# The down projection of a feed-forward as seven of eight block products, with its operands moved

## The chip, the cores and the metric

The kernel runs on one core of a Trainium2 chip. The metric is device time in microseconds (us) of one execution, the median of several runs. A core has a matrix engine (TensorE: PE for its matmuls, PEld for its weight loads), VectorE (DVE), ScalarE (ACT), GpSimd (POOL) and SyncE (SP), which here issues nearly all DMAs. Each engine works through its own list of instructions in order and waits on semaphores for the others. TensorE's results go to PSUM tiles of 128 x 512 float32, of which the kernel has eight; the other tiles lie in SBUF, 128 partitions wide.

## The reference, cut to what matters

Two layers, each with a feed-forward, a mixing sub-layer and a second feed-forward, on 512 tokens of width 1024, in float32. The feed-forward, used four times, is what changes:

```python
def _swiglu(h, wg, wu, wd):
    return (jax.nn.silu(h @ wg) * (h @ wu)) @ wd
...
    for i in range(DEPTH):
        h = _rmsnorm(x, ffn1_norm[i])
        x = x + 0.5 * _swiglu(h, ffn1_w_gate[i], ffn1_w_up[i], ffn1_w_down[i])
        h = _rmsnorm(x, mix_norm[i])
        x = x + _mixing(h, positions, w_in[i], w_out[i], fox_b, lbs[i], hgrn_norm)
        h = _rmsnorm(x, ffn2_norm[i])
        x = x + 0.5 * _swiglu(h, ffn2_w_gate[i], ffn2_w_up[i], ffn2_w_down[i])
    return _rmsnorm(x, final_norm)
```

The hidden width is 2816, 22 blocks of 128.

## The kernel before, in words

Everything is kept transposed: x is eight tiles x0 to x7 of 128 features by 512 tokens. A float32 product is made of three matmuls on operands of the rounded type fp32r: each operand is split into a rounded part (xh, wh, hh) and a rest (xl, wl, hl), and `mm3` (lines 248 to 252) adds high by high, high by low and low by high into one PSUM tile. Each weight block is loaded by SyncE into `raw` (three buffers), rounded to `wh` by ScalarE and subtracted to `wl` by VectorE (`load_split`, lines 233 to 246; two buffers each).

`ffn` (line 360) has two stages. **Gate/up**: for each of 22 blocks j, two groups (gate and up) of 8 x 3 matmuls of 512 columns into `gu_ps`; VectorE multiplies by the row factor rb, ScalarE takes the Silu, VectorE multiplies both, and the result is split into hh and hl (lines 376 to 385). **Down**: for each of the eight output blocks d, 22 x 3 matmuls of 512 columns into `d_ps`, with weights in three loads of 8, 7 and 7 blocks (line 390), and one addition of half of it to x (line 394). `after(d)` (line 395) then splits and squares that block of x for the next stage, whose first matmuls follow the last of the down stage without waiting for the norm.

The mixing stage between the feed-forwards has the same kind of projections of 512 columns (lines 250 to 252 and 425 to 427) and, among them, small matmuls in full precision (a_ps, ho_ps, ob_ps, lv_ps and others).

The order on each engine is made by the framework when the program is built: it lays out each engine's instructions by the order of the code, by when their operands can be there, and by a priority; `high_priority(AHEAD)` in `load_split` draws the splitting of weights ahead. At run time the order is fixed.

Tiles get their addresses in the order of the pools. In the built program xh, xl, wh and wl start 64 bytes past a multiple of 256, hh and hl 192 bytes past one; `pad` (48 floats) sets this.

## Time and profile before

| | us |
|---|---|
| median of 3 runs (2109.0 to 2109.46) | 2109.24 |
| profiled execution | 2108.85 |
| its span | 2107.1 |
| PE busy | 2080.3 |
| DVE busy | 993.5 |
| ACT busy | 691.6 |
| POOL busy | 13.0 |

The span is the time between the first and the last instruction of the profiled execution. A matmul's busy time contains its way through the array, which overlaps with the next one, so the busy time of PE is no sum of prices; the distance between starts is. Times inside the trace count from the start of the span.

### The profile page before, as it was taken

To read this page: it belongs to the slowest core of one execution; us is meant where nothing else is said; L and a number is where in the kernel's file an instruction comes from. 1 tells how busy PE (TensorE), PEld (TensorE's weight loads), DVE (VectorE), ACT (ScalarE), POOL (GpSimd) and SP (SyncE) were. 2 spreads that over 40 slices of the span, in tenths; PEclk is the share of its full clock that TensorE was granted. 3 is DMA by queue.
4 is the path that set the end of the run, shared out by engine and by line. 5 is a ranking of instruction groups with operands and counts; after the bars stand their busy time and mean duration, and the time that the engine had idled before them with its cause. 6 is when DMAs were issued, how large, how long until landed. Compare 5 with 4: busy or idle time off the path is not lost.

```text
span 2107.1 us, 23700 instructions
## 1 busy us (share of the span) xinstructions
PE 2080.3 (99%) x9622; PEld 1688.9 (80%) x9622; DVE 993.5 (47%) x1590; ACT 691.6 (33%) x1005; POOL 13.0 (1%) x18
## 2 busy tenths in 40 slices
PE   8999999999999999999999999999999999999997
PEld 6888888888777888888888888888887778888885
DVE  7444433556364544443344443336554554444323
ACT  5323222333353423222233322232344443323221
POOL 0000000000000000000000000000000000000000
PEclk9999999999999999999999999999999999999998
DMA  5322333211122222233332223332211122222332
GB/s 166 100 91 99 95 93 94 94 60 51 50 69 67 97 92 99 100 94 92 95 98 93 100 96 91 99 100 70 65 57 51 56 85 90 100 98 92 95 96 69
DMA packets 54373, 184.35 MB, mean 87 GB/s; under 512 B 6888, under 2 KB 7016, under 8 KB 54264
## 3 DMA queue, kind: packets, MB, share of 16 engines
q1 hardware_dynamic: 53656, 181.73, 27.1%
q8 instruction: 75, 1.23, 0.2%
q10 hardware_dynamic: 576, 1.05, 0.1%
q14 instruction: 34, 0.28, 0.0%
q0 software_dynamic: 32, 0.07, 0.0%
HBM read 180.69 MB, written 2.10 MB: 87 GB/s over the span
## 4 chain that ended last, share of the span: by engine, by line
PE 97%; DVE 2%; ACT 1%; DMA 0%; issue 0%; SPq 0%; DVEq 0%
PE gu_ps L252 15%; PE gu_ps L251 15%; PE gu_ps L250 15%; PE d_ps L252 8%; PE d_ps L250 8%; PE d_ps L251 8%; PE lv_ps L501 2%; PE sc_ps L552 2%; PE po L571 2%; PE o_ps L250 1%; PE o_ps L251 1%; PE o_ps L252 1%; PE ho_ps L680 1%; PE pt_ps L564 1%; PE v_ps L425 1%; PE v_ps L426 1%
## 5 line engine op out<-in xcount | busy, mean ns | idle before, releaser
L243 ACT CAST wh<-raw 128x1024 fp32r<-128x1024 f32 (+2 forms) x350 | 357.6, 1022 | 1112.7 <-issue 417.4
L245 DVE TENSOR_TENSOR wl<-raw,wh 128x1024 fp32r<-128x1024 f32 (+2 forms) x350 | 415.5, 1187 | 321.5 <-ACT wh L243 319.4
L250 PE MATMUL gu_ps<-xh,wh 128*128 128x512 f32 x1408 | 548.8, 390 | 7.5 <-ACT wh L243 7.5
L252 PE MATMUL gu_ps<-xh,wl 128*128 128x512 f32 x1408 | 550.4, 391 | 0.0
L251 PE MATMUL gu_ps<-xl,wh 128*128 128x512 f32 x1408 | 548.3, 390 | 0.0
L250 PEld LDWEIGHTS gu_ps<-xh,wh 128*128 128x128 f32 x1408 | 264.9, 188 | 63.6 <-ACT wh L243 7.5
L252 PEld LDWEIGHTS gu_ps<-xh,wl 128*128 128x128 f32 x1408 | 264.8, 188 | 56.1 <-issue 1.0
L251 PEld LDWEIGHTS gu_ps<-xl,wh 128*128 128x128 f32 x1408 | 264.8, 188 | 55.4 <-DVE xl L184 0.2
L252 PE MATMUL d_ps<-hh,wl 128*128 128x512 f32 x704 | 278.1, 395 | 0.0
L250 PE MATMUL d_ps<-hh,wh 128*128 128x512 f32 x704 | 278.1, 395 | 0.0
L251 PE MATMUL d_ps<-hl,wh 128*128 128x512 f32 x704 | 278.1, 395 | 0.0
L380 DVE TENSOR_TENSOR u<-gu_ps,rb 128x512 f32<-128x512 f32 x88 | 60.8, 691 | 269.2 <-PE gu_ps L252 269.0
L252 PEld LDWEIGHTS d_ps<-hh,wl 128*128 128x128 f32 x704 | 132.1, 188 | 32.2
L251 PEld LDWEIGHTS d_ps<-hl,wh 128*128 128x128 f32 x704 | 132.1, 188 | 32.1
L250 PEld LDWEIGHTS d_ps<-hh,wh 128*128 128x128 f32 x704 | 132.1, 188 | 32.1
L377 DVE TENSOR_TENSOR g<-gu_ps,rb 128x512 f32<-128x512 f32 x88 | 60.8, 691 | 178.7 <-PE gu_ps L252 176.6
L383 ACT CAST hh<-u 128x512 fp32r<-128x512 f32 x88 | 54.8, 623 | 61.2 <-DVE u L381 61.2
L394 DVE SCALAR_TENSOR_TENSOR x<-d_ps,x 128x512 f32<-128x512 f32 x32 | 22.1, 692 | 95.3 <-PE d_ps L252 95.3
L381 DVE TENSOR_TENSOR u<-u,g 128x512 f32<-128x512 f32 x88 | 60.9, 692 | 8.4
L501 PEld LDWEIGHTS lv_ps<-hQ,hk 128*128 128x128 f32 x448 | 55.8, 191 | 8.7 <-issue 5.9
L385 DVE TENSOR_TENSOR hl<-u,hh 128x512 fp32r<-128x512 f32 x88 | 60.3, 686 | 4.1 <-ACT hh L383 4.1
L571 PEld LDWEIGHTS po<-vv,pt 128*128 128x128 f32 x320 | 42.2, 190 | 19.7 <-DVE pt L569 7.8
(236 smaller groups left out, 2104.8 us busy)
## 6 DMA issues: line engine op xcount, KB each, us to landing
raw<-in_ffn_w_gate SPq DMA_DIRECT2D x88, 512.0 KB, 3.5
raw<-in_ffn_w_up SPq DMA_DIRECT2D x88, 512.0 KB, 3.5
raw<-in_w_in SPq DMA_DIRECT2D x58, 512.0 KB, 3.5
raw<-in_ffn_w_down SPq DMA_DIRECT2D x64, 448.0 KB, 3.3
raw<-in_ffn_w_down SPq DMA_DIRECT2D x32, 512.0 KB, 3.5
raw<-in_w_out_dh SPq DMA_DIRECT2D x16, 384.0 KB, 2.9
x<-in_x SPq DMA_DIRECT2D x8, 256.0 KB, 6.3
raw<-in_w_out_f SPq DMA_DIRECT2D x4, 512.0 KB, 3.6
```

Source lines behind the costliest of these rows:

```text
L243: S.copy(wh, raw)
L245: V.tensor_tensor(out=wl, in0=raw, in1=wh.bitcast(F32), op=ALU.subtract)
L250: PE.matmul(ps, lh, rh, start=first, stop=False)
L251: PE.matmul(ps, lh, rl, start=False, stop=False)
L252: PE.matmul(ps, ll, rh, start=False, stop=last)
L377: V.tensor_tensor(out=g, in0=part[0], in1=rb, op=ALU.mult)
L380: V.tensor_tensor(out=u, in0=part[1], in1=rb, op=ALU.mult)
L381: V.tensor_tensor(out=u, in0=u, in1=g, op=ALU.mult)
L383: S.copy(h1, u)
L385: V.tensor_tensor(out=h2, in0=u, in1=h1.bitcast(F32), op=ALU.subtract)
L501: PE.matmul(ps[:, e:e + 64], K[:, hh, s], Q[:, hh, s].rearrange("p (n two c) -> p n two c", two=2, c=c)[:, :, 1, :], start=True, stop=True)
L571: PE.matmul(po[:, h * HD:(h + 1) * HD], pt[:, j * 128:(j + 1) * 128], val[:, j, h * HD:(h + 1) * HD], start=j == 0, stop=j == b)
```

## The change

The down projection of two output blocks d and d + 4 at once is written as a product of 2 x 2 blocks: the weights are cut into rows d and d + 4 (the first digit of a block's name) and into the two hidden blocks of a pair (the second digit), the hidden activations into the two blocks of the pair and the two halves of the tokens, 256 columns each. Strassen's scheme makes it of seven products in place of eight. `PRODUCTS` has for each the weight blocks that are added or subtracted, the form of the activations and the places in x to which half of the result is added or subtracted.

- `hidden(p)` makes a pair of hidden blocks in one tile `uu` and, of them, seven forms: two plain halves and five sums, which GpSimd makes into `fs` (line 408). They are split into `hp` by one ScalarE and one VectorE instruction for the plain ones and one each for the sums (lines 413 and 414). There is one buffer each for `uu`, `g` and `fs`.
- `down(d, ...)` makes seven products of 256 columns for each d from 0 to 3. The four weight blocks come by four loads (into `raw` and a new tile `q`, three buffers each, line 430). Five of the seven products need a sum of two of them, made by GpSimd into `ws` (two buffers, line 443). It is then split as before (lines 445 and 447), with a third pair of wh and wl. A product's result is added to x at one or two places of 256 columns (line 460), twelve additions for each d.
- The feed-forward is done in two parts, of six and of five pairs, each with its gate/up matmuls and then its products; `hp` has six buffers. In the first d of each part the last pair's matmuls of the first two products are put behind both (`late`).
- Pools are put in another order and padded, so that xh, xl, wh, wl and hp all start at multiples of 256 bytes, in the mixing stage too. sq and dg share one buffer, rb has one, and small tiles of the mixing stage change place.
- Gate, up and the projections of the mixing stage take their eight blocks of x in the order 0, 4, 1, 5, 2, 6, 3, 7 (`KORD`), as x is now completed in pairs.

The weights' bytes are the same.

```diff
-PAD = 48
+PAD = 96
+KORD = [k for d in range(KB // 2) for k in (d, d + KB // 2)]
...
-        a = f(f"{n}_w_down").reshape(L, FB, 128, KB, 128)
-        out[f"{n}_w_down"] = a.transpose(0, 3, 2, 1, 4)
+        a = f(f"{n}_w_down").reshape(L, FB // 2, 2, 128, KB, 128)
+        out[f"{n}_w_down"] = a.transpose(0, 4, 2, 3, 1, 5)
...
-    const = ctx.enter_context(tc.tile_pool(name="const", bufs=1))
+    align = ctx.enter_context(tc.tile_pool(name="align", bufs=1))
     keep = ctx.enter_context(tc.tile_pool(name="keep", bufs=1))
     wp = ctx.enter_context(tc.tile_pool(name="wp", bufs=2))
+    const = ctx.enter_context(tc.tile_pool(name="const", bufs=1))
     small = ctx.enter_context(tc.tile_pool(name="small", bufs=2))
+    fill = ctx.enter_context(tc.tile_pool(name="fill", bufs=1))
...
-    const.tile([128, PAD], F32, name="pad")
+    align.tile([128, 32], F32, name="pad0")
+    fill.tile([128, PAD], F32, name="pad1")
...
-            sq = small.tile([128, T], F32, tag="sq", name="sq")
+            sq = small.tile([128, T], F32, tag="sq", name="sq", bufs=1)
...
-        rb = small.tile([128, T], F32, tag="rb", name="rb", bufs=2)
+        rb = small.tile([128, T], F32, tag="rb", name="rb", bufs=1)
...
+    FORMS = (("11", "22", ALU.add), ("12", "22", ALU.subtract), ("21", "11", ALU.subtract),
+             ("11", "12", ALU.add), ("21", "22", ALU.add))
+    PRODUCTS = (
+        (("11", "12"), ALU.add, 6, (("12", 0.5), ("11", -0.5))),
+        (("21", "22"), ALU.add, 5, (("21", 0.5), ("22", -0.5))),
+        (("12", "22"), ALU.subtract, 4, (("11", 0.5),)),
+        (("22",), None, 2, (("11", 0.5), ("21", 0.5))),
+        (("11", "22"), ALU.add, 0, (("11", 0.5), ("22", 0.5))),
+        (("11",), None, 1, (("12", 0.5), ("22", 0.5))),
+        (("21", "11"), ALU.subtract, 3, (("22", 0.5),)),
+    )
+    HT = T // 2
+    CHUNKS = ((0, 6), (6, 11))
     def ffn(l, wg, wu, wd, after, rb, early=None):
         with tc.tile_pool(name="ffn", bufs=1, reuse_waits="tile") as fp:
-            hh, hl = [], []
-            for j in range(FB):
-                if j == 4 and early:
-                    early()
-                part = []
-                for w in (wg, wu):
-                    wh, wl = load_split(w[l, j], KB, 128)
-                    ps = acc("gu_ps")
-                    for k in range(KB):
-                        mm3(ps, wh[:, k, :], wl[:, k, :], xh[k], xl[k], k == 0, k == KB - 1)
-                    part.append(ps)
-                g = fp.tile([128, T], F32, tag="g", name="g", bufs=2)
-                V.tensor_tensor(out=g, in0=part[0], in1=rb, op=ALU.mult)
-                S.activation(g, g, AF.Silu)
-                u = fp.tile([128, T], F32, tag="u", name="u", bufs=2)
-                V.tensor_tensor(out=u, in0=part[1], in1=rb, op=ALU.mult)
-                V.tensor_tensor(out=u, in0=u, in1=g, op=ALU.mult)
-                h1 = fp.tile([128, T], R32, name=f"hh{j}")
-                S.copy(h1, u)
-                h2 = fp.tile([128, T], R32, name=f"hl{j}")
-                V.tensor_tensor(out=h2, in0=u, in1=h1.bitcast(F32), op=ALU.subtract)
-                hh.append(h1)
-                hl.append(h2)
-            for d in range(KB):
-                ps = acc("d_ps")
-                for j0, j1 in ((0, 8), (8, 15), (15, 22)):
-                    wh, wl = load_split(wd[l, d, :, j0:j1, :], j1 - j0, 128)
+            def hidden(p):
+                uu = fp.tile([128, 2, T], F32, tag="uu", name="uu")
+                for i in range(2):
+                    part = []
+                    for w in (wg, wu):
+                        wh, wl = load_split(w[l, 2 * p + i], KB, 128)
+                        ps = acc("gu_ps")
+                        for n, k in enumerate(KORD):
+                            mm3(ps, wh[:, k, :], wl[:, k, :], xh[k], xl[k], n == 0, n == KB - 1)
+                        part.append(ps)
+                    g = fp.tile([128, T], F32, tag="g", name="g")
+                    V.tensor_tensor(out=g, in0=part[0], in1=rb, op=ALU.mult)
+                    S.activation(g, g, AF.Silu)
+                    V.tensor_tensor(out=uu[:, i, :], in0=part[1], in1=rb, op=ALU.mult)
+                    V.tensor_tensor(out=uu[:, i, :], in0=uu[:, i, :], in1=g, op=ALU.mult)
+                block = {f"{i + 1}{n + 1}": uu[:, i, n * HT:(n + 1) * HT] for i in range(2) for n in range(2)}
+                fs = fp.tile([128, len(FORMS), HT], F32, tag="fs", name="fs")
+                for i, (x0, x1, op) in enumerate(FORMS):
+                    G.tensor_tensor(out=fs[:, i, :], in0=block[x0], in1=block[x1], op=op)
+                hp = fp.tile([128, 7, 2, HT], R32, tag=f"hp{p % 6}", name=f"hp{p % 6}")
+                ends = uu.rearrange("p i (n t) -> p (i n) t", n=2)[:, 0:4:3, :]
+                for src, n0, n1 in ((ends, 5, 7), (fs, 0, 5)):
+                    S.copy(hp[:, n0:n1, 0, :], src)
+                    V.tensor_tensor(out=hp[:, n0:n1, 1, :], in0=src, in1=hp[:, n0:n1, 0, :].bitcast(F32),
+                                    op=ALU.subtract)
+                return hp
+            def down(d, p0, p1, hps):
+                n = p1 - p0
+                block = {}
+                def need(key):
+                    if key not in block:
+                        m, k = int(key[0]) - 1, int(key[1]) - 1
+                        if key in ("11", "12"):
+                            q = wp.tile([128, n, 128], F32, tag="raw", name="raw", bufs=3)
+                        else:
+                            q = fp.tile([128, n, 128], F32, tag="q", name="q", bufs=3)
+                        nc.sync.dma_start(out=q, in_=wd[l, d + m * (KB // 2), k, :, p0:p1, :])
+                        block[key] = q
+                    return block[key]
+                def weights(i):
+                    keys, op = PRODUCTS[i][:2]
+                    raw = [need(key) for key in keys]
+                    pool, sub, bufs = (fp, "f", 1) if i % 3 == 2 else (wp, "", 2)
+                    with tc.high_priority(AHEAD):
+                        src = raw[0]
+                        if op is not None:
+                            src = fp.tile([128, n, 128], F32, tag="ws", name="ws", bufs=2)
+                            G.tensor_tensor(out=src, in0=raw[0], in1=raw[1], op=op)
+                        wh = pool.tile([128, n, 128], R32, tag="wh" + sub, name="wh", bufs=bufs)
+                        S.copy(wh, src)
+                        wl = pool.tile([128, n, 128], R32, tag="wl" + sub, name="wl", bufs=bufs)
+                        V.tensor_tensor(out=wl, in0=src, in1=wh.bitcast(F32), op=ALU.subtract)
+                    return wh, wl
+                def multiply(i, ps, w, j0, j1):
+                    form = PRODUCTS[i][2]
                     for j in range(j0, j1):
-                        mm3(ps, wh[:, j - j0, :], wl[:, j - j0, :], hh[j], hl[j], j == 0, j == FB - 1)
-                V.scalar_tensor_tensor(out=x[d], in0=ps, scalar=0.5, in1=x[d], op0=ALU.mult, op1=ALU.add)
-                after(d)
+                        hi, lo = hps[j][:, form, 0], hps[j][:, form, 1]
+                        mm3(ps, w[0][:, j, :], w[1][:, j, :], hi, lo, j == 0, j == n - 1)
+                def add(i, ps):
+                    for key, f in PRODUCTS[i][3]:
+                        m, c = int(key[0]) - 1, int(key[1]) - 1
+                        xd = x[d + m * (KB // 2)][:, c * HT:(c + 1) * HT]
+                        V.scalar_tensor_tensor(out=xd, in0=ps, scalar=f, in1=xd, op0=ALU.mult, op1=ALU.add)
+                late = 2 if d == 0 else 0
+                held = []
+                for i in range(len(PRODUCTS)):
+                    w = weights(i)
+                    ps = acc("d_ps")[:, 0:HT]
+                    if i < late:
+                        multiply(i, ps, w, 0, n - 1)
+                        held.append((i, ps, w))
+                        if i < late - 1:
+                            continue
+                    else:
+                        multiply(i, ps, w, 0, n)
+                        add(i, ps)
+                    for i1, ps1, w1 in held:
+                        multiply(i1, ps1, w1, n - 1, n)
+                        add(i1, ps1)
+                    held = []
+            for p0, p1 in CHUNKS:
+                hps = []
+                for p in range(p0, p1):
+                    if p == 2 and early:
+                        early()
+                    hps.append(hidden(p))
+                for d in range(KB // 2):
+                    down(d, p0, p1, hps)
+                    if p1 == FB // 2:
+                        after(d)
+                        after(d + KB // 2)
...
-            for k in range(KB):
-                mm3(ps, wh[:, k, :], wl[:, k, :], xh[k], xl[k], k == 0, k == KB - 1)
+            for n, k in enumerate(KORD):
+                mm3(ps, wh[:, k, :], wl[:, k, :], xh[k], xl[k], n == 0, n == KB - 1)
```

The order on VectorE where the first feed-forward passes from gate/up to down, before (u and hl of the last block j = 21; d_ps of d = 0):

```order
L380 TENSOR_TENSOR u_1889<-gu_ps_1861,rb_186 128x512
L245 TENSOR_TENSOR wl_1931<-raw_1927,wh_1929 128x896
L381 TENSOR_TENSOR u_1889<-u_1889,g_1886 128x512
L385 TENSOR_TENSOR hl21_1894<-u_1889,hh21_1892 128x512
L245 TENSOR_TENSOR wl_1958<-raw_1954,wh_1956 128x896
L245 TENSOR_TENSOR wl_1993<-raw_1989,wh_1991 128x1024
L394 SCALAR_TENSOR_TENSOR x0_74<-d_ps_1896,x0_74 128x512
```

and now, at the end of the first part (uu, fs and hp5 belong to its last pair, ws to the sums of weights, d_ps_1201 and d_ps_1227 are the first two products):

```order
L447 TENSOR_TENSOR wl_1199<-ws_1195,wh_1197 128x768
L447 TENSOR_TENSOR wl_1257<-ws_1253,wh_1255 128x768
L403 TENSOR_TENSOR uu_1045<-gu_ps_1150,rb_193 128x512
L447 TENSOR_TENSOR wl_1225<-ws_1221,wh_1223 128x768
L404 TENSOR_TENSOR uu_1045<-uu_1045,g_1175 128x512
L414 TENSOR_TENSOR hp5_1186<-uu_1045,hp5_1186 128x2x256
L460 SCALAR_TENSOR_TENSOR x0_81<-d_ps_1201,x0_81 128x256 x2
L414 TENSOR_TENSOR hp5_1186<-fs_1180,hp5_1186 128x5x256
L447 TENSOR_TENSOR wl_1281<-q_1219,wh_1279 128x768
L447 TENSOR_TENSOR wl_1308<-ws_1304,wh_1306 128x768
```

A weight's subtract stands between the two multiplications in both. What followed them was the split of one block; now it is that of the two plain halves, then the additions of the first product, then the split of the five sums.

On GpSimd, which had nothing there before, in the same place (ws sums of weights, fs sums of activations):

```order
L443 TENSOR_TENSOR ws_1221<-q_1217,q_1219 128x768
L408 TENSOR_TENSOR fs_1180<-uu_1045 128x256
L443 TENSOR_TENSOR ws_1253<-raw_1193,q_1219 128x768
L443 TENSOR_TENSOR ws_1304<-raw_1191,q_1219 128x768
L443 TENSOR_TENSOR ws_1356<-q_1217,raw_1191 128x768
L408 TENSOR_TENSOR fs_1180<-uu_1045 128x256 x4
L443 TENSOR_TENSOR ws_1386<-raw_1382,raw_1384 128x768
L443 TENSOR_TENSOR ws_1417<-q_1413,q_1415 128x768
```

Two weight sums for later products stand ahead of the last four sums of the last pair.

On TensorE, the first use of the last hidden block, before (in the first d, behind 63 matmuls on earlier blocks):

```order
L250 MATMUL d_ps_1896<-hh20_1820,wh_1956 128x512
L251 MATMUL d_ps_1896<-hl20_1822,wh_1956 128x512
L252 MATMUL d_ps_1896<-hh20_1820,wl_1958 128x512
L250 MATMUL d_ps_1896<-hh21_1892,wh_1956 128x512
L251 MATMUL d_ps_1896<-hl21_1894,wh_1956 128x512
L252 MATMUL d_ps_1896<-hh21_1892,wl_1958 128x512
```

and now that of the last pair's sums (d_ps_1259 is the third product, behind 36 matmuls of the first two and 15 of its own):

```order
L257 MATMUL d_ps_1259<-hp4_1040,wl_1257 128x256
L255 MATMUL d_ps_1259<-hp5_1186,wh_1255 128x256
L255 MATMUL d_ps_1283<-hp0_335,wh_1279 128x256
L256 MATMUL d_ps_1259<-hp5_1186,wh_1255 128x256
L257 MATMUL d_ps_1259<-hp5_1186,wl_1257 128x256
L256 MATMUL d_ps_1283<-hp0_335,wh_1279 128x256
L255 MATMUL d_ps_1310<-hp0_335,wh_1306 128x256
L256 MATMUL d_ps_1310<-hp0_335,wh_1306 128x256
L257 MATMUL d_ps_1283<-hp0_335,wl_1281 128x256
```

Matmuls of the fourth and fifth product stand between those of the third on the last pair.

## Rows read from the trace of the kernel before

**Rows 1.** The page, busy time and share by engine; granted clock by slices

```profile
PE 2080.3 (99%) x9622; PEld 1688.9 (80%) x9622; DVE 993.5 (47%) x1590; ACT 691.6 (33%) x1005; POOL 13.0 (1%) x18
PEclk9999999999999999999999999999999999999998
```

**Rows 2.** The page, chain that ended last, share of the span by engine

```profile
PE 97%; DVE 2%; ACT 1%; DMA 0%; issue 0%; SPq 0%; DVEq 0%
```

**Rows 3.** Groups by line on TensorE: count, busy us, mean ns, idle before

```profile
L252 PE MATMUL gu_ps<-xh,wl 128*128 128x512 f32 x1408 | 550.4, 391 | 0.0
L252 PE MATMUL d_ps<-hh,wl 128*128 128x512 f32 x704 | 278.1, 395 | 0.0
```

**Rows 4.** Windows of one tile (PE, PEld, DVE busy, clock): gu_ps, then d_ps

```profile
710.00:910.00 200.00, 200.00 (x884) 165.62 (x883) 25.54 (x37) 1.00 0.29 95
...
930.00:1040.00 110.00, 110.00 (x473) 88.51 (x472) 4.84 (x7) 1.00 0.33 97
```

**Rows 5.** Windows of the four down stages: PE, PEld, DVE, ACT, POOL

```profile
251.70:374.90 123.20, 123.20 (x529) 99.10 (x528) 42.37 (x47) 32.86 (x40) 0.95 (x1) 1.00 0.32 95
1967.30:2090.50 123.20, 123.20 (x529) 98.87 (x527) 36.51 (x39) 28.95 (x33) 0.00 (x0) 1.00 0.28 78
sum 492.70, PE 492.70 PEld 396.15 DVE 163.61 ACT 127.50 POOL 1.91; mean PE 123.17 PEld 99.04 DVE 40.90 ACT 31.88 POOL 0.48
```

**Rows 6.** Chain in order of time, mixing stage: start, us, what, count

```profile
403.52 1.76 PE a_ps L482 x16
452.44 0.90 PE ho_ps L680 x8
...
510.77 0.43 PE ob_ps L536 x2
```

**Rows 7.** Groups by line and shape on VectorE

```profile
L245 DVE TENSOR_TENSOR wl<-raw,wh 128x1024 fp32r<-128x1024 f32 x270 | 330.3, 1223 | 201.1 <-ACT wh L243 200.9
L245 DVE TENSOR_TENSOR wl<-raw,wh 128x896 fp32r<-128x896 f32 x64 | 69.9, 1092 | 111.3 <-ACT wh L243 109.4
...
L394 DVE SCALAR_TENSOR_TENSOR x<-d_ps,x 128x512 f32<-128x512 f32 x32 | 22.1, 692 | 95.3 <-PE d_ps L252 95.3
...
L245 DVE TENSOR_TENSOR wl<-raw,wh 128x768 fp32r<-128x768 f32 x16 | 15.3, 958 | 9.1 <-ACT wh L243 9.1
...
L576 DVE TENSOR_TENSOR o<-po,den 128x256 f32<-128x256 f32 x16 | 6.8, 423 | 15.4 <-PE po L571 15.2
```

**Rows 8.** Groups by line and shape on ScalarE

```profile
L243 ACT CAST wh<-raw 128x1024 fp32r<-128x1024 f32 x270 | 283.8, 1051 | 854.7 <-issue 318.1 <-PE gu_ps L251 259.6 <-PE d_ps L251 132.7
...
L383 ACT CAST hh<-u 128x512 fp32r<-128x512 f32 x88 | 54.8, 623 | 61.2 <-DVE u L381 61.2
...
L243 ACT CAST wh<-raw 128x768 fp32r<-128x768 f32 x16 | 13.4, 835 | 26.3 <-issue 8.9 <-PE o_ps L251 5.5 <-PE fk_ps L252 5.0
```

**Rows 9.** Groups by line and shape on GpSimd

```profile
L278 POOL CAST lev<-lev_f 128x448 uint8<-128x448 f32 x1 | 0.8, 780 | 21.4 <-DMA lev_f<-in_c_lev 21.4
```

**Rows 10.** The page, DMA issues: KB each, us to landing

```profile
raw<-in_ffn_w_down SPq DMA_DIRECT2D x64, 448.0 KB, 3.3
```

**Rows 11.** Timeline, from gate/up to down: start, us, engine, what

```profile
251.50 0.39 PE L252 MATMUL gu_ps<-xh,wl 128*128 128x512 f32 x1
251.72 0.40 PE L250 MATMUL d_ps<-hh,wh 128*128 128x512 f32 x1
...
251.92 0.69 DVE L380 TENSOR_TENSOR u<-gu_ps,rb 128x512 f32<-128x512 f32 x1 [3.31 <-PE gu_ps L252]
...
253.73 0.68 DVE L381 TENSOR_TENSOR u<-u,g 128x512 f32<-128x512 f32 x1
...
254.44 0.62 ACT L383 CAST hh<-u 128x512 fp32r<-128x512 f32 x1 [1.76 <-DVE u L381]
...
255.10 0.69 DVE L385 TENSOR_TENSOR hl<-u,hh 128x512 fp32r<-128x512 f32 x1 [0.69 <-ACT hh L383]
```

More of the change, by code (lines that the diff above doesn't have):

```diff
@@ L221, in norm_finish @@
         r = norm_rows(nrm)
-        dg = small.tile([128, NB, 128], F32, tag="sq", name="dg")
+        dg = small.tile([128, NB, 128], F32, tag="sq", name="dg", bufs=1)
         for b in range(NB):
@@ L274, in late_constants @@
         nc.sync.dma_start(out=masks, in_=a["c_masks"])
-        with tc.tile_pool(name="levp", bufs=1) as lp:
-            t = lp.tile([128, len(LEVELS), 1, 64], F32, name="lev_f")
-            nc.sync.dma_start(out=t[:, :, 0, :], in_=a["c_lev"])
-            G.tensor_copy(lev, t)
+        t = small.tile([128, len(LEVELS), 1, 64], F32, tag="sq", name="lev_f", bufs=1)
+        nc.sync.dma_start(out=t[:, :, 0, :], in_=a["c_lev"])
+        G.tensor_copy(lev, t)
         nc.sync.dma_start(out=fbias[0:4, :], in_=a["fox_forget_bias"])
@@ L439, in mixing @@
         at = [lines(mp, [128, 8], tag=f"ad{p}", name=f"ad{p}") for p in range(2)]
+        hss = [lines(mp, [128, NB, 2], tag=f"hss{p}", name=f"hss{p}") for p in range(2)]
         def put_out(kind, b, o, n):
@@ L660, in mixing @@
         ho = [slot(f"ho{b}", (128, 4, 128), f"ho{b}") for b in range(NB)]
-        hss = [lines(mp, [128, NB, 2], tag=f"hss{p}", name=f"hss{p}") for p in range(2)]
         hrs = [None, None]
@@ L683, in states @@
                                            op0=ALU.mult, op1=ALU.add)
[L684 removed]
+                    sq = mp.tile([128, 128], F32, tag="ca", name="hsq", bufs=1)
                     S.activation(sq, ho[b][:, h, :], AF.Square, accum_out=hss[p][:, b, hh:hh + 1])
```

1 line of the change is left out of this document (removed).

## The prediction

> **What bounds the kernel now.** I read the page's busy shares first, then the chain of waits, then the groups by line, and last the windows of single stages. TensorE is busy 99% of the span at full granted clock, 2.4 GHz [rows 1], and 97% of the chain that ended last is its matmuls [rows 2]: the kernel takes as long as its matmul stream. "Busy" here includes the pipelined tail of each matmul (391 ns and 395 ns in [rows 3]), so the price of one more or one fewer is the distance between starts, from the windows: in 200 us of gate/up 884 matmuls are counted, two of them at the edges, 200/882 = 226.8 ns each; in 110 us of the down stage 473, so 110/471 = 233.5 ns [rows 4]. The down projection runs four times, 123.2 us each, with TensorE busy throughout; the four windows sum to 492.7 us [rows 5].
>
> The profiled execution took 2108.85 us (span 2107.1 and 1.75 around it), 0.39 under the median of the three runs shown, 2109.24. A measurement of this kernel can tell about 0.2%, 4 us, from no change.
>
> **The change, part by part.**
>
> *Matmuls of the down projection.* Before: 4 stages x 8 d x 22 j x 3 = 2112 of 512 columns (3 x 704 in [rows 3]). After: 4 stages x 4 d x 11 pairs x 7 products x 3 = 3696 of 256 columns, 7/8 of the columns but 1.75 times the instructions and weight loads. The trace has no 256-column matmul on rounded operands, so I bound its price. From below by [rows 6]: a 1-column matmul with its weight load takes 1.76/16 = 110 ns, a 128-column full-precision one, which streams for as long as 256 rounded columns, 0.90/8 = 112.5 ns. So a load and a matmul together do not go under 110 ns. From above: 512 columns at 2.4 GHz are 213.3 ns, so the down stage shows 20.2 ns beside them and gate/up 13.5. If that were a fixed part of every instruction, 256 columns would cost 106.7 + 13.5 = 120 or 106.7 + 20.2 = 126.9 ns. I take half of the gate/up row, 113.4 ns, because the operands now have equal alignment, as in gate/up, and because it lies next to the 112.5 measured on an equally long stream. 3696 x 0.1134 = 419.1 us against 492.7: **-73.6 us** (ends: 406.6 at 110 ns, -86.1; 469.0 at 126.9 ns, -23.7).
>
> *The other engines in the stage.* Per d of a six-pair part TensorE takes 7 x 18 x 0.1134 = 14.3 us, of a five-pair part 11.9. VectorE subtracts seven weight blocks, 958 ns at 768 columns [rows 7]; at 640, by the slope between the 896 and the 768 rows (134 ns per 128), 824. It adds twelve 256-column results to x, each near 423 ns [rows 7]. That is 6.7 + 5.1 = 11.8 us under 14.3, and 5.8 + 5.1 = 10.9 under 11.9. ScalarE's seven casts at 835 ns [rows 8] are 5.8 us. GpSimd has five sums per d, twenty per part. Its only elementwise row here is a cast of 448 columns in 780 ns [rows 9], 1.74 ns a column. A sum reads two operands, so I bound it by one cast and two casts: 1.34 to 2.67 us at 768 columns, 1.11 to 2.23 at 640; five of them 6.7 to 13.4 us beside 14.3, and 5.6 to 11.1 beside 11.9. All of this fits beside TensorE, so I cost it at nothing; the cover is a margin of only 1.0 us per d on VectorE in the five-pair part. If that is gone, TensorE waits for weights in every product. The four loads per d (384 or 320 KB, the 448 KB one takes 3.3 us [rows 10]) are issued a whole d ahead on SP's queue; nothing there comes to wait. In gate/up a pair takes 96 x 0.2268 = 21.8 us; VectorE's four subtracts, four multiplications and two splits are 4.9 + 2.8 + 0.7 + 1.5 = 9.9 of them, and `uu` and `fs`, one buffer each, are read out some 9 us after a pair ends, while the next writes `uu` after 10.9. That costs nothing.
>
> *The two starts of the down product in each feed-forward.* Before, its first matmul follows the last gate/up matmul after 0.22 us, because the last hidden block is needed only at j = 21; its split ends at 255.79 [rows 11]. Now the last pair must pass five sums before the split. Count from the last gate/up matmul of a six-pair part, in the order shown above. VectorE multiplies by rb (0.69), does a weight subtract that stands between (0.96) and multiplies by g (0.69): 2.34 us. ScalarE rounds the two plain blocks (0.62) and VectorE subtracts (0.69): 3.65. TensorE has 30 matmuls on earlier pairs, 3.4 us, then waits only 0.3, and after those six has 15 more: it stands at 5.9 us. GpSimd must first do a weight sum (released at 1.65, so until about 3.4), then four sums of 256 columns. At a third above the cast's rate these are 0.59 each: 5.8. Then one rounding of 1280 columns (1.25 x 1051 ns = 1.3 [rows 8]) and its subtract (1.25 x 1223 = 1.5 [rows 7]): 8.6 us. TensorE has a few matmuls to fill in, so it loses 8.6 - 5.9 plus what the next weights are late, less those: about 3 us. The five-pair part covers less on TensorE and gets there earlier: also about 3. Eight starts: **+24 us** (0 if the sums were free, 48 if they cost two casts each).
>
> *Alignment elsewhere.* Gate, up and the projections of the mixing stage (4224, 3 x 1408 in [rows 3], and, by the order, 1776 matmuls of 512 columns) move from 64 bytes past a multiple of 256 to none. The trace shows that position matters: 226.8 ns where both operands stand at 64, 233.5 where they differ by 128 [rows 4]. It does not show what an aligned pair costs. Bounds: 215 ns, the 512 cycles of one full-precision 256-column matmul (0.43/2 in [rows 6]), and 233.5. Only the difference between the operands is seen to matter, and that stays zero: I take **0** (ends -71 and +40 us).
>
> *The rest.* The order of k in gate/up lets the blocks d and d+4, which now end together, be used last: the last addition to x is 0.42 us instead of 0.69 [rows 7]. Single buffers for sq, dg and rb only bind between stages: 0.
>
> Sum: 2108.9 - 73.6 + 24 = **2059 us**.
>
> **Rivals.**
>
> *A. Alignment pays on every matmul.* The 13.5 ns beside the 213.3 would be the price of starting 64 bytes off, and go. 6000 x 11.8 = 71 us less, and the products at 112.5: 2059 - 71 - 3 = 1985; with half of it 2022. For it: 226.8/213.3 is 17/16, as if one more piece of 128 bytes were read. Against: no aligned pair in this trace.
>
> *B. GpSimd and VectorE shut each other out, at a moderate price.* If a sum and a weight subtract could not run together, a six-pair and a five-pair d together would need 5(s6 + s5) + 6.7 + 5.8 us, against TensorE's 26.2. That binds from 1.95 ns a column for a sum; at 2.15, about midway between this point and that of C, s6 = 1.65 and s5 = 1.38 make 27.7 us, 16 times is 443, 24 more than TensorE: 2083, some 2070 to 2105. For it: both engines read the same raw blocks, and GpSimd's busy time before, 13 us [rows 1], shows nothing of it. The Trainium skill, "SBUF — State Buffer", section "Who interferes with whom", says that a VectorE instruction with two SBUF inputs and a GpSimd instruction that reads SBUF fully block each other; no run shown here bears it out or denies it. The price is in "GPSIMD Engine Reference", section "Performance versus the Vector engine": 4497 ns for a sum of 2048 columns, 2.2 ns a column, by which the time would come to an estimated 2087.
>
> *C. The same lock with dearer sums: slower.* Its place is the down stage, its price the sum. Above 2.38 ns a column (s6 = 1.83) the two d take 29.3 us, the stages 469, and with the 24 us of the starts the gain is gone. At two casts a sum 37.0 us, 592, so 2232. Each 0.1 us on a sum costs 16 us. Against: it lies in the upper half of the bounds, and needs the lock as well.
>
> That the change does not take away an eighth of the down columns can be excluded: the order shows 3696 of 256.
>
> **How the numbers follow.** My forecast 0.40 (own range 2040 to 2105, by the dearer matmul price); A 0.23; B 0.22; C 0.15. Faster: 0.37 of mine, all of A, 0.17 of B: 0.77. Same: 0.01 + 0.03: 0.04. Slower: 0.02 + 0.02 + 0.15: 0.19. The range 1985 to 2112 takes in the forecast with its bounds, the weaker half of A, and B; about 0.2 is left out.
>
> **What would show it.** Right: the distance of the products' matmuls near 113 ns in a window inside a down stage; a gap of some 3 us on TensorE behind the first 51 or 42 matmuls of each part, released by hp; POOL busy 300 to 400 us; gate/up at 226.8 still. A shows as 215 to 220 in gate/up. B and C show as VectorE subtracts and GpSimd sums longer than their sizes ask, and TensorE waiting for wh or wl inside products. I am wrong if TensorE stands still in mid-stage, or if 256 columns cost 120 ns or more.

## The result, and the profile after

| | before | after |
|---|---|---|
| median of the runs, us | 2109.12 (4 runs) | 2228.03 (4 runs) |
| profiled execution, us | 2108.85 | 2226.59 |
| its span, us | 2107.1 | 2224.4 |

The ratio is 1.0566, with a 95% interval from 1.0546 to 1.0586: slower by 119 us, where 50 us faster was forecast.

The page of the kernel after: busy time by engine, the granted clock by slices, the chain that ended last:

```profile
PE 2097.0 (94%) x11206; PEld 1776.6 (80%) x11206; DVE 1338.0 (60%) x2070; ACT 795.6 (36%) x1131; POOL 539.6 (24%) x398
...
PEclk9999999998999999999999999999999999999998
...
PE 2%; DVE 1%; POOL 0%; ACT 0%; issue 0%; DVEq 0%; ACTq 0%
```

Against [rows 1] TensorE's share fell from 99 to 94%, VectorE rose from 47 to 60 and GpSimd from 13 us to 540. The chain breaks off after 3% of the span, so it can't be read as [rows 2] could; the stages have to be read one by one.

Windows of the eight down parts (six pairs and five pairs in turn): us, busy time of PE, PEld, DVE, ACT and POOL, granted clock, DMA share, GB/s:

```profile
147.20:224.30 77.10, 65.70 (x506) 63.89 (x505) 59.60 (x79) 24.10 (x29) 35.45 (x21) 0.96 0.29 87
333.20:401.40 68.20, 57.72 (x422) 54.43 (x421) 58.92 (x89) 28.73 (x42) 32.26 (x22) 0.95 0.23 69
...
sum 582.20, PE 495.07 PEld 476.48 DVE 468.11 ACT 207.99 POOL 269.88; mean PE 61.88 PEld 59.56 DVE 58.51 ACT 26.00 POOL 33.73
```

That answers to [rows 5]: 582.2 us against 492.7, so 89.5 of the 117.7 us between the two profiled executions are lost where 73.6 were to be won. TensorE is not busy for 87 of the 582 us (its busy time counts a matmul's way through the array), and VectorE is busy for 468, where it had been for about a third of the stage. The mixing stages take 324.5 and 321.2 us against 311.2 and 310.9, 23.6 more, and gate/up of the four feed-forwards 4.9 more, 4.4 of them in the first, whose cause no run looked for. 89.5 + 23.6 + 4.9 make 118.0: nothing else of size is missing.

Inside a down part, counted from the starts of all 3696 matmuls in the trace: 3696 x 120.0 ns make 443.5 us; gaps of TensorE add 105 us, 40 of them at the eight starts and 65 later; some 340 matmuls come 213 ns apart instead of 120, which, with a few at the edges of these stretches, adds 33. That sums to 582.

The groups by line on TensorE, count, busy us, mean ns, idle before and what ended most of it; they answer to [rows 3]:

```profile
L257 PE MATMUL gu_ps<-xh,wl 128*128 128x512 f32 x1408 | 550.5, 391 | 0.7 <-DVE wl L250 0.6
L257 PE MATMUL d_ps<-hp,wl 128*128 128x256 f32 x1232 | 364.3, 298 | 52.3 <-DVE wl L447 51.8
```

The products wait for `wl`, the weight's rest that VectorE subtracts. Groups of VectorE and GpSimd, shapes apart, against [rows 7, 9]:

```profile
L460 DVE SCALAR_TENSOR_TENSOR x<-d_ps,x 128x256 f32<-128x256 f32 x384 | 144.3, 415 | 29.0 <-PE d_ps L257 28.1
L447 DVE TENSOR_TENSOR wl<-ws,wh 128x768 fp32r<-128x768 f32 x80 | 108.1, 1351 | 45.0 <-ACT wh L445 44.3
...
L443 POOL TENSOR_TENSOR ws<-raw,q 128x768 f32<-128x768 f32 x32 | 58.6, 1830 | 41.7 <-DVE wl L447 41.7
...
L414 DVE TENSOR_TENSOR hp<-uu,hp 128x512 fp32r<-128x512 f32 x44 | 55.7, 1265 | 5.5 <-ACT hp L413 5.5
...
L443 POOL TENSOR_TENSOR ws<-q 128x768 f32<-128x768 f32 x16 | 29.6, 1850 | 28.9 <-DVE wl L447 21.2 <-issue 7.7
...
L447 DVE TENSOR_TENSOR wl<-q,wh 128x640 fp32r<-128x640 f32 x16 | 28.5, 1779 | 0.0
```

A subtract of 768 columns, 958 ns in [rows 7], takes 1351 on average, one of 640 columns 1779 in one place, the split of 512 columns 1265 instead of 692. The addition x<-d_ps, which reads one operand from PSUM, stays at 415 ns. These are means over all, beside a sum or not. Counted in the trace, the 54 subtracts of 768 columns here that run while GpSimd has a sum in hand take 1908 ns on average, the 58 others 954; the additions take 415 (238 of them) and 416 (146). Why is seen in the timeline at the first start, the stretch that [rows 11] show of before (start, duration, engine, line, operation, idle before):

```profile
147.89 1.84 POOL L443 TENSOR_TENSOR ws<-raw,q 128x768 f32<-128x768 f32 x1 [1.94 <-DVE wl L447]
...
148.33 2.22 DVE L447 TENSOR_TENSOR wl<-ws,wh 128x768 fp32r<-128x768 f32 x1
...
150.47 0.68 DVE L404 TENSOR_TENSOR uu<-uu,g 128x512 f32<-128x512 f32 x1
...
150.60 0.39 PE L257 MATMUL d_ps<-hp,wl 128*128 128x256 f32 x1 [1.26 <-DVE wl L447]
150.62 2.21 POOL L443 TENSOR_TENSOR ws<-q,raw 128x768 f32<-128x768 f32 x1 [0.89 <-DVE wl L447]
...
151.83 1.56 DVE L414 TENSOR_TENSOR hp<-uu,hp 128x512 fp32r<-128x512 f32 x1 [0.69 <-ACT hp L413]
...
152.79 3.27 POOL L408 TENSOR_TENSOR fs<-uu 128x256 f32<-128x256 f32 x4
...
156.10 1.26 ACT L413 CAST hp<-fs 128x1280 fp32r<-128x1280 f32 x1 [4.30 <-POOL fs L408]
...
157.41 0.39 PE L255 MATMUL d_ps<-hp,wh 128*128 128x256 f32 x1 [1.32 <-ACT hp L413]
```

The subtract begins at 148.33 while the sum runs until 149.73, and ends 0.82 us behind it: nearly its whole work comes after the sum. It goes the other way too: the sum at 150.62 begins while VectorE multiplies two SBUF operands (150.47 to 151.15) and takes 2.21 us instead of 1.84. The split at 151.83 then begins while that sum runs until 152.83, and ends 0.56 us behind it. The same at the change to the second d:

```profile
169.86 1.57 ACT L445 CAST wh<-ws 128x768 fp32r<-128x768 f32 x2 [3.66 <-POOL ws L443]
...
170.73 0.96 DVE L447 TENSOR_TENSOR wl<-ws,wh 128x768 fp32r<-128x768 f32 x1 [1.83 <-ACT wh L445]
...
171.76 1.81 POOL L443 TENSOR_TENSOR ws<-raw,q 128x768 f32<-128x768 f32 x1 [1.94 <-DVE wl L447]
...
171.94 2.45 DVE L447 TENSOR_TENSOR wl<-ws,wh 128x768 fp32r<-128x768 f32 x1
...
174.44 0.38 PE L257 MATMUL d_ps<-hp,wl 128*128 128x256 f32 x1 [2.33 <-DVE wl L447]
```

After the gaps of the start the clock falls. Windows of the same part, before and behind 163.4:

```profile
159.80:163.20 3.40, 3.40 (x16) 3.40 (x17) 2.68 (x5) 0.39 (x1) 2.42 (x1) 0.53 0.56 151
163.40:171.40 8.00, 8.00 (x69) 8.00 (x68) 5.30 (x9) 3.07 (x4) 3.71 (x2) 1.00 0.15 40
```

In the first the granted clock is about half (0.53), the 1.2 GHz level, and 16 matmuls take 3.4 us; before it, TensorE had stood five times between 149 and 159. In the second the clock is full again, and 69 matmuls, two of them at the edges, take 8.0 us.

### The profile page after: what moved, and what is told of

The parts are those of the page before. It is cut to its first block, busy times and chain, and to the rows that moved or that the text cites. A ratio compares the mean times of both kernels' runs of the same rounds, so it can differ in the third digit from the quotient of the medians.

```text
span 2224.4 us, 28385 instructions
## 1 busy us (share of the span) xinstructions
PE 2097.0 (94%) x11206; PEld 1776.6 (80%) x11206; DVE 1338.0 (60%) x2070; ACT 795.6 (36%) x1131; POOL 539.6 (24%) x398
## 5 line engine op out<-in xcount | busy, mean ns | idle before, releaser
L408 POOL TENSOR_TENSOR fs<-uu 128x256 f32<-128x256 f32 x220 | 240.5, 1116 | 1112.5 <-DVE uu L404 1100.6
L248 ACT CAST wh<-raw 128x1024 fp32r<-128x1024 f32 (+1 forms) x254 | 263.1, 1036 | 546.3 <-PE gu_ps L256 325.9
L257 PE MATMUL d_ps<-hp,wl 128*128 128x256 f32 x1232 | 364.3, 298 | 52.3 <-DVE wl L447 51.8
L255 PE MATMUL d_ps<-hp,wh 128*128 128x256 f32 x1232 | 363.3, 296 | 28.1 <-ACT hp L413 14.3
L256 PE MATMUL d_ps<-hp,wh 128*128 128x256 f32 x1232 | 360.8, 294 | 6.7 <-DVE hp L414 6.7
L250 DVE TENSOR_TENSOR wl<-raw,wh 128x1024 fp32r<-128x1024 f32 (+1 forms) x254 | 306.1, 1205 | 82.4 <-ACT wh L248 82.0
L257 PEld LDWEIGHTS d_ps<-hp,wl 128*128 128x128 f32 x1232 | 249.0, 203 | 60.8 <-DVE wl L447 60.6
L255 PEld LDWEIGHTS d_ps<-hp,wh 128*128 128x128 f32 x1232 | 248.3, 202 | 36.1 <-ACT wh L445 17.9
L256 PEld LDWEIGHTS d_ps<-hp,wh 128*128 128x128 f32 x1232 | 249.3, 203 | 9.4 <-DVE hp L414 9.1
L447 DVE TENSOR_TENSOR wl<-ws,wh 128x768 fp32r<-128x768 f32 (+1 forms) x160 | 182.5, 1142 | 73.9 <-ACT wh L445 72.9
L445 ACT CAST wh<-ws 128x768 fp32r<-128x768 f32 (+1 forms) x160 | 123.3, 779 | 287.3 <-PE d_ps L256 141.4
L460 DVE SCALAR_TENSOR_TENSOR x<-d_ps,x 128x256 f32<-128x256 f32 x384 | 144.3, 415 | 29.0 <-PE d_ps L257 28.1
L401 DVE TENSOR_TENSOR g<-gu_ps,rb 128x512 f32<-128x512 f32 x88 | 60.6, 688 | 132.2 <-PE gu_ps L257 129.3
```

The lines of the kernel that those rows point to most:

```text
L248: S.copy(wh, raw)
L250: V.tensor_tensor(out=wl, in0=raw, in1=wh.bitcast(F32), op=ALU.subtract)
L255: PE.matmul(ps, lh, rh, start=first, stop=False)
L256: PE.matmul(ps, lh, rl, start=False, stop=False)
L257: PE.matmul(ps, ll, rh, start=False, stop=last)
L408: G.tensor_tensor(out=fs[:, i, :], in0=block[x0], in1=block[x1], op=op)
```

## The experiments

### The mixing stage: a shared buffer

A small edit of the change, one of the "small tiles of the mixing stage", puts the square `hsq` of the mixing stage into the buffer of `ca`, a temporary of the rotary step. **Theory:** `ca` can then be written only behind the last `hsq`, which starts the small products of the dilated attention later. **Rival:** the moved addresses or the order of k.

e1, on the kernel after:

```diff
-                    sq = mp.tile([128, 128], F32, tag="ca", name="hsq", bufs=1)
+                    sq = mp.tile([128, 128], F32, tag="hsq", name="hsq", bufs=1)
```

> The changed kernel with hsq in a buffer of its own again (it had been put into that of ca). Theory: the mixing stage lost 13 and 10 us because the rope of the dilated heads writes ca and now waits until the last hsq of the states is made, so the transposes of its result (dt_ps) start some 20 us later; with its own buffer both mixing stages are back at 311 us and the time falls by 23 to about 2204. Rival: the mixing stage is slower because its tiles moved or because the clock falls there; then the time stays within 5 us of 2228.

Measured: 2202.82, ratio 1.0444 (1.0413 to 1.0474); the mixing stages take 310.4 and 310.3 us. e2 is the reverse edit on the kernel before:

> The kernel before with that one edit: hsq in the buffer of ca. Theory: 2109 + 23 = 2132, the clock at half for some microseconds in each mixing stage. Rival: no difference, 2109.

Measured: 2139.4. One word of code costs 25 us in the one kernel and 30 in the other. Windows of the first mixing stage after, and then in e1, 20 us each:

```profile
520.00:540.00 20.00, 18.81 (x106) 15.69 (x105) 10.27 (x24) 4.58 (x8) 0.00 (x0) 1.00 0.18 54
540.00:560.00 20.00, 15.14 (x57) 11.71 (x57) 7.28 (x33) 7.46 (x21) 0.00 (x0) 0.57 0.00 1
```

```profile
520.00:540.00 20.00, 19.90 (x123) 17.08 (x122) 14.65 (x44) 7.03 (x10) 0.00 (x0) 1.00 0.17 54
540.00:560.00 20.00, 20.00 (x105) 15.35 (x105) 9.01 (x31) 11.21 (x35) 0.00 (x0) 1.00 0.14 37
```

With the shared buffer TensorE first runs out of work and then goes at half clock. The trace has the first `ca` at 552.3 us of the span in the kernel after, and at 525.7 in e1.

### The sums: a lock, or too slow an engine?

**Theory:** while GpSimd reads SBUF for a sum, a VectorE instruction with two SBUF operands stands still, and the other way round. **Rival:** the sums are only long, and late in a chain from sum to `wh` to `wl`. e3 leaves the sums of weights out (each product takes its first block):

```diff
-                        if op is not None:
+                        if False:
```

> The changed kernel without the sums of weight blocks: each product takes its first block alone (the output is another one); matmuls, casts, subtracts and loads stay. Theory (VectorE's subtracts and GpSimd's sums shut each other out, and the gap of 2.5 us at the second product of each d comes of it): these gaps go, subtracts are back at 958 and 824 ns, the down stages come from 145 to about 119 us for each feed-forward (924 matmuls at 120 ns and some 8 us at the two starts), so 2228 - 105 = about 2120. Rival (VectorE and ScalarE are too full by themselves, or their order is wrong): the gaps stay and the time is above 2190.

Measured: 2118.7. The loss comes with the sums, but both readings still fit. e4 and e5 keep something on GpSimd in the sums' place that writes and doesn't read; e5's edit, of which e4 has two lines:

```diff
-                            G.tensor_tensor(out=src, in0=raw[0], in1=raw[1], op=op)
+                            G.memset(src, 0.0)
+                            G.memset(src, 0.0)
+                            G.memset(src, 0.0)
```

> The changed kernel with each sum of weights replaced by two memsets of the same buffer on GpSimd (the output is another one): about 1.45 us in place of 1.84 at 768 columns, with the same waits and the same places, but nothing is read. Theory (the lock is on reading): subtracts at 958 and 824 ns, most of the gaps go, about 2135. Rival (the round from sum to cast to subtract, two buffers deep, is simply too long): gaps of about 2 us stay at each d and the time is above 2190.

Measured: 2116.3. But two memsets are shorter than a sum, so:

> The changed kernel with each sum of weights replaced by three memsets of the same tile (the products then take zero weights, so the output is not the reference's). Two memsets take GpSimd 1.4 us on average in the run with two, less than the 1.85 us of a sum, so that run left open whether the sums are only too slow. Three take some 2.06 us, longer than a sum, and keep GpSimd's queue and the chain from sum to wl in place, but read nothing. If the loss comes from GpSimd reading while VectorE reads two operands, no gap of 2 us comes back at the start of each d and the time stays within 10 us of the 2116 with two. If the length of the sum in the chain is the cause, the gaps are as in the changed kernel or larger: about 2200 to 2240.

Measured: 2126.5, some 100 us less than the kernel after; gaps of 0.4 us are left at two of the three later d of a six-pair part and at one d of three five-pair parts. Groups of e5, shapes apart, and a subtract beside a memset in its timeline:

```profile
L449 DVE TENSOR_TENSOR wl<-ws,wh 128x768 fp32r<-128x768 f32 x80 | 77.9, 983 | 21.8 <-ACT wh L447 20.7
...
L443 POOL MEMSET ws<- 128x768 f32 x80 | 59.1, 740 | 464.6 <-PE pt_ps L663 380.5 <-DVE wl L449 84.1
```

```profile
172.36 0.74 POOL L445 MEMSET ws<- 128x768 f32 x1
...
172.52 0.96 DVE L449 TENSOR_TENSOR wl<-ws,wh 128x768 fp32r<-128x768 f32 x1 [0.53 <-ACT wh L447]
```

Three memsets keep GpSimd for 2.2 us, longer than the 1.85 us of a sum, and the subtract is back at 983 ns on average. Of all 112 subtracts of 768 columns in the down parts, the 64 that run beside memsets alone take 955 ns on average, the 40 beside nothing 957; only the 8 that meet a sum of activations, which reads, take 1433. So it is not the length of the sums: it is that GpSimd reads while VectorE reads two operands. (Memsets also don't wait for the loaded blocks; inside the first part of the kernel after, the trace's waits of GpSimd for `ws` are for `wl`, 28.4 us, not for loads. And e4 and e5 give TensorE weights of zero in five of seven products; e3, whose weights are not zero, comes within 8 us of e5, so that isn't what makes them fast.)

This is the rule of the Trainium skill, "SBUF — State Buffer", section "Who interferes with whom": a VectorE instruction with two SBUF inputs contends with a GpSimd instruction that reads SBUF, not with one that only writes it, and one with at most one SBUF input, outside certain modes named there, doesn't contend. The traces agree in all three points: the subtract takes 1908 ns beside sums and 955 beside memsets, and the addition, which has one input in PSUM, 415 in the kernel after and 418 in e12, where there are no sums of weights.

e9 takes the sums of weights to VectorE, the busier engine, on top of e1:

```diff
-                            G.tensor_tensor(out=src, in0=raw[0], in1=raw[1], op=op)
+                            V.tensor_tensor(out=src, in0=raw[0], in1=raw[1], op=op)
```

> The kernel of e1_own_hsq (2203) with the five sums of weights for each d made by VectorE in place of GpSimd, the sums of activations left on GpSimd. VectorE is the busier engine already and gets 7 + 5 instructions of 0.96 us and 12 additions of 0.42: 16.6 us for each d of a six-pair part against 15.1 of matmuls at 120 ns, and 15.0 against 12.6 in a five-pair part. If the two engines shut each other out, this still wins: four stages of 4 x 16.6 + 4 x 15.0 = 126.4, 506 us with VectorE as the bound, and some 20 for the eight starts, against 577 before: about 2150. If they ran freely beside each other and GpSimd's own pace was the limit, VectorE's load would grow for nothing and the time would be above 2200.

Measured: 2173.9, 29 us faster than e1 though VectorE has more to do. Windows of the first six-pair and the first five-pair part:

```profile
147.70:214.40 66.70, 62.08 (x505) 60.72 (x504) 60.56 (x96) 24.39 (x29) 3.92 (x4) 1.00 0.33 100
...
323.60:395.30 71.70, 58.95 (x421) 56.80 (x420) 60.63 (x107) 29.84 (x43) 3.85 (x5) 0.90 0.23 67
```

The six-pair parts take 66.8 to 68.3 us. That this is close to the 66.4 worked out (4 x 16.6) is luck: VectorE does not bound them. What is over 504 x 0.12 = 60.5 us is lost to gaps in the first d and to half clock behind them; in the later ones TensorE has no gap over 0.2 us. The reason is in the starts of VectorE's instructions. Where one follows the other at once, it starts some 0.08 us before the other ends, so that a subtract or sum of 768 columns takes 0.87 us of its time and an addition 0.33, and a d costs it 12 x 0.87 + 12 x 0.33 = 14.4 us, under the 15.1 of the matmuls. The first three five-pair parts take 72 to 73 where 60 was expected. Groups of VectorE in the first of those (323.5 to 395.3):

```profile
L460 DVE SCALAR_TENSOR_TENSOR x<-d_ps,x 128x256 f32<-128x256 f32 x47 | 17.5, 417 | 2.2 <-PE d_ps L257 2.2
L447 DVE TENSOR_TENSOR wl<-ws,wh 128x640 fp32r<-128x640 f32 x18 | 14.8, 821 | 5.4 <-ACT wh L445 5.3
L443 DVE TENSOR_TENSOR ws<-raw,q 128x640 f32<-128x640 f32 x7 | 5.7, 818 | 0.0
L189 DVE SCALAR_TENSOR_TENSOR xl<-x,par,xh 128x512 fp32r<-128x512 f32 x7 | 5.2, 747 | 0.5 <-ACT xh L187 0.5
L199 DVE TENSOR_TENSOR ss<-ss,sq 128x512 f32<-128x512 f32 x5 | 3.4, 686 | 0.0
```

I had left out `after(d)`: two splits xl and two sums ss for each d. By the distances between starts (0.74 at 640 columns, 0.33, 0.66 and 0.60 us) a d costs VectorE 12 x 0.74 + 12 x 0.33 + 2 x 0.66 + 2 x 0.60 = 15.4 us, more than the 12.6 of the matmuls. But that is 61.6 for the part, and VectorE is busy for 60.6 of its 71.7 us. Of the 21 us that the part takes over its 50.4 of matmuls, TensorE's gaps are 15, of which 10.3 end with an addition that frees a result tile, and 63 matmuls at half clock add 6. So VectorE's load is a part of the loss and the order in its queue another; no run tells them apart. (The last part, which no split xl follows, takes 65.)

e10 and e11 divide the sums: two on VectorE, three on GpSimd, and all sums of activations on VectorE.

```diff
-                    G.tensor_tensor(out=fs[:, i, :], in0=block[x0], in1=block[x1], op=op)
+                    V.tensor_tensor(out=fs[:, i, :], in0=block[x0], in1=block[x1], op=op)
...
-                            G.tensor_tensor(out=src, in0=raw[0], in1=raw[1], op=op)
+                            (V if i in (1, 2) else G).tensor_tensor(out=src, in0=raw[0], in1=raw[1], op=op)
```

> The kernel of e1_own_hsq with the sums of the second and third product made by VectorE, the other three by GpSimd, and the sums of activations by VectorE. By mutual exclusion the time in which only one of the two engines can work is 3 x 1.85 + 9 x 0.96 = 14.2 us for a six-pair d (in the changed kernel 5 x 1.85 + 7 x 0.96 = 16.0) against 15.1 of matmuls, and VectorE's own 9 x 0.96 + 12 x 0.42 = 13.7; for a five-pair d 12.1 and 12.5 against 12.6. If throughput under the lock is what counts, the gaps at each d nearly vanish: stages near 490 in all, about 2115. If it is the order and length of the chain from sum to wl at each d's start, gaps of about a microsecond stay: 2130 to 2180.

Measured: 2154.4, better than either engine alone, in the range given for the chain. Six-pair parts take 67.3 to 68.6 us with gaps of 1.9 and 1.4 us left at the third and fourth d, so totals below TensorE's don't suffice. The first three five-pair parts take 68 to 69. There the sums left out `after(d)` again: by the distances VectorE's own work is 9 x 0.74 + 12 x 0.33 + 2.5 = 13.1 us for each d, against 12.6, besides three sums on GpSimd. e11 has `(0, 1)` in place of `(1, 2)`:

> The same with the first and second product's sums on VectorE. The engines' totals are those of e10: if throughput decides, the same time within 10 us; if the chain at the start of each d decides, this one is the faster, as both products that the start of a d waits for then have no GpSimd sum, by up to 30 us.

Measured: 2166.2, 12 us slower than e10 (one run of each; the four of the kernel after lie within 8 us). The expectation that it would be the faster fell. The six-pair parts became slower (71.4 us, with a gap of 1.9 at each later d) and the first three five-pair parts faster (66), so the order matters, and differently in the two; what makes the rest of the gaps stays open.

### The alignment alone, and the price of 256 columns

e6 and e7 take the kernel before and move its operands only (e7 keeps `PAD` at 48 and has the other two lines):

```diff
-PAD = 48
+PAD = 96
...
+    fill = ctx.enter_context(tc.tile_pool(name="fill", bufs=1))
...
+    fill.tile([128, 32], F32, name="pad1")
```

> The kernel before with the alignment of the change alone: all rounded operands at multiples of 256 bytes, nothing else moved. If only the difference between the operands of a matmul counts, the 2112 matmuls of the down stage go from 233.5 to 226.7 ns, 14.3 us, and the 384 of the mixing stage's last projection by some 5 ns, 1.9 us: 2093. If the positions made no difference to time: 2109. If absolute alignment paid (215 ns), 1985 to 2022, which gate/up of the changed kernel already speaks against.

Measured: 2094.03, ratio 0.9928 (0.9914 to 0.9941).

> The kernel before with hidden blocks moved by 128 bytes, so that both operands of every rounded matmul stand 64 bytes past a multiple of 256. If only the difference counts, the same time as with multiples of 256: 2093 within 3 us. If a start at a multiple of 256 is worth something in itself, this one stays above it.

Measured: 2094.04, ratio 0.9929 (0.9916 to 0.9943). At 0 and at 64 the time is the same, so it is not the start at a multiple of 256. The difference of 128 between the operands is what is left to explain the 233.5 ns; no run has both at 192, so that an operand at 192 is slow by itself is not excluded. Gate/up of the kernel after, with both operands at 0, keeps the 226.8 ns that it had at 64 in [rows 4], 100/441 (window of `gu_ps`):

```profile
742.00:842.00 100.00, 100.00 (x443) 82.84 (x442) 12.42 (x18) 1.00 0.33 97
```

e8 adds to e6 that each matmul of the down stage is issued as two halves:

```diff
-                ps = acc("d_ps")
+                pss = [acc("d_ps")[:, 0:256] for _ in range(2)]
...
-                        mm3(ps, wh[:, j - j0, :], wl[:, j - j0, :], hh[j], hl[j], j == 0, j == FB - 1)
+                        for i, ps in enumerate(pss):
+                            c = slice(i * 256, i * 256 + 256)
+                            mm3(ps, wh[:, j - j0, :], wl[:, j - j0, :], hh[j][:, c], hl[j][:, c],
+                                j == 0, j == FB - 1)
...
+                for i, ps in enumerate(pss):
+                    c = slice(i * 256, i * 256 + 256)
+                    V.scalar_tensor_tensor(out=x[d][:, c], in0=ps, scalar=0.5, in1=x[d][:, c],
+                                           op0=ALU.mult, op1=ALU.add)
```

> The kernel before with aligned operands and each matmul of the down stage issued as two of 256 columns, no sums anywhere. If the 13.3 ns beside the streaming time belong to each instruction, 4224 x 120.0 = 506.9 us against 2112 x 226.7 = 478.8: 28 us over the aligned kernel, about 2121. If they go with the columns, as my 113.4 ns had it, 4224 x 113.4 = 479: no difference, about 2093.

Measured: 2121.45, 27.4 over e6. Windows of `d_ps` in e6 and then in e8:

```profile
255.00:355.00 100.00, 100.00 (x443) 82.81 (x442) 4.15 (x6) 1.00 0.32 96
```

```profile
260.00:360.00 100.00, 100.00 (x835) 100.00 (x835) 4.71 (x12) 1.00 0.31 92
```

100/441 = 226.8 ns for 512 columns, and 100/833 = 120.0 ns for 256, where nothing else differs. Halving the columns leaves 13.3 ns beside the 106.7 of streaming, so at full clock it is a price of each matmul with its weight load; which of the two has it is not shown. At half clock it is gone: in the kernel after, 213 ns for 256 columns are 256/1.2, and the few matmuls of 512 columns in such a stretch (`v_ps`) come 427 ns apart, 512/1.2. What makes the 13.3 ns stays open.

### What is left without the sums

e12 joins the edits of e1 and e3.

> The kernel of e1_own_hsq without the sums of weights (each product takes the first of its weight blocks, so the output is not the reference's): the nearest thing to seven products whose sums cost nothing. If the loss of the changed kernel is the sums beside VectorE, the shared buffer and the price of 120 ns, this is 2118.7 less the 24 of the buffer: 2095, no better than the kernel before with aligned operands alone (2094), although it has an eighth fewer columns. If a seven-product scheme had kept a gain that only the sums eat, it would lie near my forecast of 2059 with the buffer taken out, 2040 to 2070.

Measured: 2091.62, ratio 0.9922 (0.9905 to 0.9938), which can't be told from e6. Windows of its first two down parts:

```profile
146.50:210.80 64.30, 62.90 (x504) 62.08 (x503) 46.88 (x78) 24.41 (x29) 3.28 (x4) 0.97 0.34 98
319.80:375.00 55.20, 53.03 (x421) 52.16 (x420) 47.91 (x90) 29.51 (x43) 3.35 (x5) 0.97 0.30 83
```

With its starts as they are (20 us of gaps at the eight starts, and 6 at half clock), the scheme would come with free sums of weights only to what a few lines of padding bring the kernel before. The versions that beat both kernels and keep the result are e6 and e7, by 0.7%.

## Why the prediction was wrong

From the 2059 forecast to the 2226.6 of the profiled execution, by the prediction's own steps:

| step of the prediction | forecast | measured | difference |
|---|---|---|---|
| "I take half of the gate/up row, 113.4 ns" | 419.1 us | 3696 x 120.0 = 443.5 | +24 |
| two starts in each feed-forward | +24 | 40 of gaps | +16 |
| other engines: "All of this fits beside TensorE, so I cost it at nothing" | 0 | 65 of gaps at later d | +65 |
| (not foreseen) half clock behind gaps | 0 | 33 | +33 |
| "The rest": single buffers and moved tiles, 0 | 0 | 23.6, mixing | +24 |
| gate/up | 0 | 4.9, of which 4.4 in the first feed-forward | +5 |

These make 167, against 167.6 between the two times. Both signs that the prediction named for being wrong came: TensorE stands still in mid-stage, and 256 columns cost 120 ns.

- **The step that failed** is the one on the other engines, "All of this fits beside TensorE": the work was added up for each engine alone. A sum on GpSimd and a subtract on VectorE exclude each other (e5), and the sums cost 1.85 us at 768 and 1.57 at 640 columns, inside the bounds of one and two casts. (Undisturbed sums of 256, 640 and 768 columns take 0.73, 1.56 and 1.84 us: 2.2 ns a column and some 0.2 us for each sum, which a price by column alone leaves out.) Together for a six-pair d: 5 x 1.85 + 7 x 0.96 = 16.0 us, against 15.1 of matmuls at 120 ns. For a five-pair d: 5 x 1.57 + 7 x 0.82 + 2.9 = 16.5, against 12.6. By the distances between VectorE's starts they are 15.4 and 15.6, still over. The 2.9 are the four instructions of `after(d)`, which the step "10.9 under 11.9" left out. That alone did no harm: the "margin of 1.0 us" is gone by durations (13.8), but by distances VectorE has 7 x 0.74 + 12 x 0.33 + 2.5 = 11.7 us, and in e12, without sums of weights, TensorE has no gap over 0.2 us behind the first d.
- **Rival C** had the mechanism, the sign and, at 1.83 us, the point from which the gain is gone; the sums lie just past it. By its formula, 5 x (1.85 + 1.57) + 12.5 = 29.6 for two d, the stages would take 474 us and the kernel 2114. The runs showed more than totals: each engine waits for the other in a chain (GpSimd 210 us for `wl` in the whole run), TensorE stands at each d, and then the clock halves. C's chance of 0.15 was too low by an error of mine, too: its point, 2.38 ns a column, lies below the middle of the bounds of 1.74 and 3.48, not "in the upper half".
- **The matmul price.** The upper bound that the prediction gave for a fixed part, 120 ns, was the value. The row that it preferred, 112.5 ns for a full-precision matmul of 128 columns, has the same streaming time but isn't the same instruction. The Trainium skill, "TensorE: Matmul & The Clock Gate", section "Back-to-back issue gap", has 262 cycles for 256 columns as the gap of an isolated matmul, at 2.4 GHz an estimated 109 ns; the 120.0 of e8, in a stream of weight loads and matmuls, differ from it, and the measurement decides.
- **The starts.** The steps came in the order foreseen. The first gap comes sooner, behind the 17th matmul, since `wl` of the second product is held up by a sum (148.33 above); the four sums of the last pair take 3.27 us instead of 4 x 0.59, and a start costs 5 us instead of 3.
- **Alignment elsewhere, 0**, was right, and rival A falls: e6 and e7 give the same time at 0 and at 64, and gate/up of the kernel after, with both operands at 0, stays at 226.8 ns. The prediction used the equal alignment in its price of a product, but didn't see that it was the part of the change worth having by itself: 15 us.
- **The rest, 0**, was wrong by one line. I read the buffers that the change made single, and not that two tags became one.

## What to carry to other kernels

Add up work that two engines do on SBUF as if one engine did it, where GpSimd reads and VectorE reads two operands; then count whatever else VectorE has to do in that stage. Take an engine's load from the distances between its starts, not from its durations. Fewer columns in smaller instructions pay only beyond what each instruction costs besides them: here, at full clock, 13.3 ns beside 106.7, so seven eighths of the columns are 93% of the aligned time (443.5 of 478.8 us), not 87.5%. Try the cheap part of a large change alone first.

## What the runs showed that I had not expected

- The time of a rounded matmul depends on where its operands start: 226.8 ns with both at 0 or both at 64 modulo 256, 233.5 with one at 64 and the other at 192 [rows 4]. In the latter case the single distances alternate, 229 and 238 ns.
- A gap has a second price: behind some of the gaps of a down part TensorE ran at half the granted clock, 213 ns for each matmul instead of 120, 33 us in all, beside the gaps' own 105.
- One shared buffer of 64 KB for two small temporaries cost 25 us of 2200, and again a part of it by the clock (0.57 granted in 20 us).
